# Residual updates of a decoder step: work moved from GpSimd to VectorE and handed out behind the critical tiles

## The chip, the cores and the metric

One Trainium2 chip, one core. The engines that the text names are PE (TensorE: matrix products; PEld is its loading of weights), VectorE (DVE in the rows), ScalarE (ACT), GpSimd (POOL) and SyncE (SP, which only issues DMAs here). Each runs its own instructions strictly in its order; they meet through semaphores. The metric is the device time of one execution in microseconds. Before the change it is 1234.71 us, the median of three runs (1232.79 to 1235.05).

## The reference

One step of a two-layer decoder over 320 tokens (256 of a prompt, 8 times 8 of samples), width 1024. Layer 0 mixes with an S5 state space and a GLU, layer 1 with latent attention (MLA); each layer then attends to 256 memory tokens and applies an MLP. Every sublayer is normalised before and after, and this is what the change touches:

```python
def rms_norm(x, g):
    y = x * lax.rsqrt(jnp.mean(x * x, axis=-1, keepdims=True) + EPS)
    return y * g
...
hp = hp + rms_norm(yp, norm_mix_post[i])
hp = hp + rms_norm(mem_attend(rms_norm(hp, norm_mem_pre[i]), mk, mv, w_mem_q[i], w_mem_o[i]), norm_mem_post[i])
hp = hp + rms_norm(sq_relu_mlp(rms_norm(hp, norm_mlp_pre[i]), w_mlp_up[i], w_mlp_down[i]), norm_mlp_post[i])
```

So between two dense stages stands: a norm of the output y, an addition to the residual h, and the norm of the new h, whose result the next stage multiplies by its weights.

## The kernel before

**Layout.** Activations lie transposed, channels on 128 partitions and the 320 tokens along the row, in KD = 8 tiles j of 128 x 320. Products keep nearly full float32 precision by three matmuls: weights and activations are each split into a rounded high part and a remainder, and `mm3` (L202) adds high x high, high x low and low x high. The activations of a stage are thus `xh` and `xl`, the weights `whi` and `wlo`. `load_chunk` (L178) brings a chunk of 128 x 1024 weights by SyncE's queue into `wraw`, makes `whi` on ScalarE (L190) and `wlo` on VectorE (L191), or on GpSimd for the chunks numbered 3 and 5 after an update (`POOL_LO`, L85). `dense` (L208) goes over groups of up to four output blocks, for each over the chunks of the contraction, and then has a function `evac` take the sums out of PSUM.

**Update.** After the last matmul of a stage, the sum of the squares of its output gives, through a matmul with ones (`ss`) and a square root on ScalarE, the tile `rt` (root of the mean square, one value per token). Four of the five updates are `update_scaled` (L263). It doesn't divide by rt, but works with the residual times rt: for each j it makes the product t_up = h x rt (L272; VectorE for j = 0 and 1, GpSimd for the other six), the sum s = y x gain + t_up (L274, VectorE, written over y), xh = s x gain (L278, ScalarE; L276, VectorE, for j = 0) and xl (L279, VectorE). PE can start on tile j of the next stage when xh and xl of that tile are there. The scale rt goes out again in the next norm. For that, the squares of s (`stat_add`, L111: squares on ScalarE, additions on GpSimd, L118) are summed, `ex` (L284) is the epsilon times rt squared, and `next_root` (L294) makes the root. Where h is needed later (`restore`), it is made as s divided by rt: a reciprocal on VectorE (L160) and eight products on GpSimd (L289). The fifth is `update` (L249), in front of the latent stage of MLA: it divides by rt at once, and the root of the new h (L261) follows in it.

**The five stretches.** They are called A to E here. A is the update after the GLU, in front of the memory query of layer 0 (from 228 us on in the trace). B follows the memory attention, in front of the MLP of layer 0 (361 us). C is `update` after that MLP, in front of MLA (614 us). D follows MLA, in front of the memory query of layer 1 (855 us), and E is in front of the last MLP (979 us); E restores nothing and instead turns h into rows by token as filler work for PE. PE has other filler work too: transposes of cached keys (`kt`, copied to `ktb` by VectorE, L1107, and ScalarE) in A and D, the keys and values of the memory of layer 1 in B.

**What sets the order.** The program is written as a sequence of operations, and a scheduler puts each engine's instructions into an order by the times that it reckons for them. `tc.issue_after(x)` holds back the operations inside it until x has been issued in that reckoning. `self.hold` uses it for weight chunks: chunk n waits in the order for the instruction that is put down for it. In the memory query (`mem_attention`, L1112) the root of h is wanted only for the softmax scale `rsc` (L1165), and stands in before behind the first of two groups, four blocks wide (L1154). In the MLP (`mlp`, L1280) it is wanted after the first half (L1304); there `evac` squares the relu (L1297) and makes `hl` (L1298).

Of the kernel before, what the change touches and what calls it, by code (L numbers as in the profile page):

```python
# [84 lines left out]
POOL_LO = (3, 5)  # L85
# [3 lines left out]
class Trunk:  # L89
# [88 lines left out]
    def load_chunk(self, srcs, cols):  # L178
# [12 lines left out]
        (nc.gpsimd if self.chunk in POOL_LO else nc.vector).tensor_sub(lo[:, :cols], raw[:, :cols], hi[:, :cols].bitcast(F32))  # L191
        return hi, lo

# [55 lines left out]
    def update(self, y, rt, gpost, stat=True):  # L249
# [3 lines left out]
        st = self.stat_new()  # L253
        for j in range(KD):
            t = self.small("t_up", bufs=2)
            (nc.vector if j < 2 else nc.gpsimd).tensor_mul(t, y[:, j, :], r)  # L256
            nc.vector.scalar_tensor_tensor(h[:, j, :], t, gpost(j), h[:, j, :], op0=ALU.mult, op1=ALU.add)  # L257
            if stat:
                self.stat_add(st, h[:, j, :], nc.gpsimd)
        if stat:  # L260
            self.r_next, self.rt_next = self.rsqrt(self.stat_sum(st), D)  # L261

    def update_scaled(self, y, rt, gpost, gpre, restore=True):  # L263
# [4 lines left out]
        self.chunk, self.hold, self.first_sum = 0, {3: self.gate}, self.summed  # L268
        st = self.stat_new()
        for j in range(KD):  # L270
            t = self.small("t_up", bufs=2)
            scaled = (nc.vector if j < 2 else nc.gpsimd).tensor_mul(t, h[:, j, :], rt)  # L272
            s = y[:, j, :]
            nc.vector.scalar_tensor_tensor(s, s, gpost(j), t, op0=ALU.mult, op1=ALU.add)  # L274
            if j == 0:
                nc.vector.tensor_scalar(xh[:, j, :], s, gpre(j), None, op0=ALU.mult)  # L276
            else:
                nc.scalar.activation(xh[:, j, :], s, AF.Copy, scale=gpre(j))  # L278
            lo = nc.vector.scalar_tensor_tensor(xl[:, j, :], s, gpre(j), xh[:, j, :].bitcast(F32),  # L279
                                                op0=ALU.mult, op1=ALU.subtract)  # L280
            self.stat_add(st, s, nc.gpsimd)
        with self.tc.issue_after(lo.ins):
            ex = self.small("w_r", bufs=1)
            nc.vector.scalar_tensor_tensor(ex, rt, EPS, rt, op0=ALU.mult, op1=ALU.mult)  # L284
            r = self.inverse(rt) if restore else None
        if restore:
            with self.tc.issue_after(scaled.ins):
                for j in range(KD):
                    nc.gpsimd.tensor_mul(h[:, j, :], y[:, j, :], r)  # L289
        self.pending = st, ex  # L290
        if not restore:
            self.fillers = self.h_to_tokens(y, rt)

    def next_root(self):  # L294

        st, ex = self.pending
# [19 lines left out]
    def build(self):  # L316
        tc, nc, I, O = self.tc, self.nc, self.I, self.O
        with ExitStack() as ctx:
# [11 lines left out]
            self.fillers = []  # L330
            cp = self.cp
# [1471 lines left out]
```

## Time and profile before

| | |
|---|---|
| median of the runs | 1234.71 us (1232.79 to 1235.05) |
| the profiled execution | 1235.15 us, of which the span of the profile is 1233.5 us |
| PE busy | 1139.3 us, 92% of the span |
| PE weight load busy | 1026.6 us, 83% |
| VectorE busy | 726.7 us, 59% |
| ScalarE busy | 546.7 us, 44% |
| GpSimd busy | 182.3 us, 15%, 190 instructions |
| mean granted clock of PE | 0.966 of full speed |

The shares are means over the whole span, and the stages differ. GpSimd is idle for most of it and dense in the five stretches. PE waits little elsewhere, so its idle time there and the few stretches in which its granted clock was half of the full one are what an update can cost. In the rows further below, a square bracket behind an instruction gives the idle time of its engine just before it and, behind the arrow, the instruction that ended that idle time.

### The profile page before, as it was taken

How to read it: one execution, taken by the hardware profiler on the slowest of the kernel's cores; microseconds unless marked ns; L12 is line 12 of the kernel's file. 1: busy time of each engine (PE TensorE's matmuls, PEld its weight loads, DVE VectorE, ACT ScalarE, POOL GpSimd, SP SyncE). 2: the span in 40 equal slices, each digit the busy share in tenths (PEclk: the TensorE clock that was granted, in tenths of full speed). 3: DMA queues.
4: the chain of work that ended last, by engine and by line, in shares of the span. 5: the costliest groups of instructions: out<-in, count | busy, mean ns of one | idle time of the engine just before them, and what ended most of it. 6: DMA issues, size and time to landing. Idle time of an engine off the chain costs nothing.

```text
span 1233.5 us, 21037 instructions
## 1 busy us (share of the span) xinstructions
PE 1139.3 (92%) x8105; PEld 1026.6 (83%) x8105; DVE 726.7 (59%) x1266; ACT 546.7 (44%) x992; POOL 182.3 (15%) x190
## 2 busy tenths in 40 slices
PE   4997699889988999999989999998999899999996
PEld 3886599776787999999979984578967899999996
DVE  5998944664468553564587674416843685435543
ACT  6344454534444543453366353224443365335541
POOL 2000000350027000000050054202700140000011
PEclk8999799999998999999999999989999999999998
DMA  8535358637334445454443565437272434454441
GB/s 165 180 100 116 72 118 289 245 120 269 124 103 126 137 154 153 143 151 152 154 143 104 170 185 153 140 137 268 84 272 94 137 99 144 151 153 139 155 149 49
DMA packets 151233, 184.84 MB, mean 150 GB/s; under 512 B 16719, under 2 KB 119388, under 8 KB 151068
## 3 DMA queue, kind: packets, MB, share of 16 engines
q1 hardware_dynamic: 141660, 174.84, 46.3%
q10 hardware_dynamic: 6976, 5.46, 1.4%
q0 software_dynamic: 2496, 3.20, 0.9%
q8 instruction: 64, 1.05, 0.3%
q14 instruction: 37, 0.30, 0.1%
HBM read 174.89 MB, written 6.21 MB: 147 GB/s over the span
## 4 chain that ended last, share of the span: by engine, by line
PE 75%; DVE 10%; DMA 5%; SPq 3%; issue 2%; ACT 2%; POOL 2%; POOLq 0%; DVEq 0%; ACTq 0%
PE mm L205 17%; PE mm L204 17%; PE mm L206 17%; PE kt L102 2%; PE sps L1182 2%; PE mm L567 2%; DVE xl L279 2%; PE s L1662 2%; SPq L944 2%; DVE wlo L191 1%; DMA natc<-in_ssm_c_im 1%; PE pov L1239 1%; PE s L1703 1%; PE pps L1217 1%; PE mm L569 1%
## 5 line engine op out<-in xcount | busy, mean ns | idle before, releaser
L191 DVE TENSOR_TENSOR wlo<-wraw,whi 128x1024 fp32r<-128x1024 f32 (+1 forms) x206 | 252.9, 1232 | 279.3 <-ACT whi L190 269.1
L190 ACT ACTIVATE whi<-wraw 128x1024 fp32r<-128x1024 f32 (+1 forms) x216 | 224.5, 1044 | 302.8 <-PE mm L205 246.6
L205 PE MATMUL mm<-xl,whi 128*128 128x320 f32 x944 | 296.8, 317 | 9.1 <-DVE xl L279 7.0
L204 PE MATMUL mm<-xh,whi 128*128 128x320 f32 x944 | 280.6, 318 | 12.7 <-ACT t_up L1295 3.6
L206 PE MATMUL mm<-xh,wlo 128*128 128x320 f32 x944 | 287.3, 314 | 0.0
L205 PEld LDWEIGHTS mm<-xl,whi 128*128 128x128 f32 x944 | 181.8, 193 | 13.7 <-DVE xl L279 9.6
L204 PEld LDWEIGHTS mm<-xh,whi 128*128 128x128 f32 x944 | 175.9, 192 | 16.8 <-ACT t_up L1295 3.9
L206 PEld LDWEIGHTS mm<-xh,wlo 128*128 128x128 f32 x944 | 179.7, 192 | 0.1
L204 PE MATMUL mm<-hh,whi 128*128 128x320 f32 x512 | 158.2, 309 | 0.0
L205 PE MATMUL mm<-hl,whi 128*128 128x320 f32 x512 | 158.0, 309 | 0.0
L206 PE MATMUL mm<-hh,wlo 128*128 128x320 f32 x512 | 157.1, 308 | 0.0
L205 PEld LDWEIGHTS mm<-hl,whi 128*128 128x128 f32 x512 | 96.1, 188 | 0.0
L204 PEld LDWEIGHTS mm<-hh,whi 128*128 128x128 f32 x512 | 96.1, 188 | 0.0
L206 PEld LDWEIGHTS mm<-hh,wlo 128*128 128x128 f32 x512 | 95.9, 188 | 0.0
L118 POOL TENSOR_TENSOR sq<-sq 128x320 f32<-128x320 f32 x34 | 41.4, 1219 | 204.1 <-ACT sq L120 203.4
L191 POOL TENSOR_TENSOR wlo<-wraw,whi 128x1024 fp32r<-128x1024 f32 x10 | 25.4, 2538 | 286.4 <-ACT whi L190 198.1
L102 PEld LDWEIGHTS kt<-ident,kn 128*128 128x128 f32 x256 | 28.9, 143 | 22.2 <-issue 5.8
L102 PE MATMUL kt<-ident,kn 128*128 128x128 f32 x256 | 38.1, 283 | 8.6 <-ACT ktb L1109 3.2
L1591 POOL DMA_DIRECT2D rop<-in_cache_k_rope x64 | 34.5, 540 | 37.4 <-issue 20.4
L256 POOL TENSOR_TENSOR t_up<-y,rr 128x320 f32<-128x320 f32 x6 | 7.5, 1258 | 219.2 <-DVE h L257 219.2
L1107 DVE COPY ktb<-kt 128x512 f32<-128x512 f32 x32 | 22.0, 687 | 21.0 <-PE kt L102 20.9
L1109 ACT ACTIVATE ktb<-kt 128x512 f32<-128x512 f32 x32 | 19.1, 596 | 31.4 <-PE kt L102 26.0
(495 smaller groups left out, 1958.6 us busy)
## 6 DMA issues: line engine op xcount, KB each, us to landing
wraw<-in_w_mlp_up SPq DMA_DIRECT2D x64, 512.0 KB, 4.2
wraw<-in_w_mlp_down SPq DMA_DIRECT2D x64, 512.0 KB, 3.5
kn<-in_cache_mem_k SPq DMA_DIRECT2D x16, 1024.0 KB, 7.3
vn<-in_cache_mem_v SPq DMA_DIRECT2D x16, 1024.0 KB, 9.1
wraw<-in_w_glu SPq DMA_DIRECT2D x32, 256.0 KB, 4.1
wraw<-in_w_mem_q SPq DMA_DIRECT2D x16, 512.0 KB, 5.3
wraw<-in_w_mem_o SPq DMA_DIRECT2D x16, 512.0 KB, 5.0
lat<-in_cache_kv_latent SPq DMA_DIRECT2D x64, 128.0 KB, 2.5
```

The costliest lines, as they stand in the source:

```text
L102: self.nc.tensor.transpose(out, in_, self.ident[b:b + k, b:b + k])
L118: eng.tensor_add(st['acc'], st['acc'], st['last'])
L190: nc.scalar.activation(hi[:, :cols], raw[:, :cols], AF.Copy)
L191: (nc.gpsimd if self.chunk in POOL_LO else nc.vector).tensor_sub(lo[:, :cols], raw[:, :cols], hi[:, :cols].bitcast(F32))
L204: nc.tensor.matmul(ps, wh, xh, start=start, stop=False)
L205: nc.tensor.matmul(ps, wh, xl, start=False, stop=False)
L206: nc.tensor.matmul(ps, wl, xh, start=False, stop=stop)
L279: lo = nc.vector.scalar_tensor_tensor(xl[:, j, :], s, gpre(j), xh[:, j, :].bitcast(F32), op0=ALU.mult, op1=ALU.subtract)
L567: nc.tensor.matmul(ps[b][:, :MT], w[:, bs], xh[:, k, :], start=k == 0, stop=k == KD - 1)
L944: nc.sync.dma_start(tt[s * K:(s + 1) * K, s:], kk[:, 0:L - s])
L1182: nc.tensor.matmul(sps[h * 32:(h + 1) * 32, :MT], qm[:, h * 2 + db, j * 128 + i * 32:j * 128 + (i + 1) * 32], ktb[:, h * 2 + db, :], start ...
L1591: last[eng] = eng.dma_start(dst, src[bass.ds(v, 1)].rearrange("o p d -> (o p) d"))
```

## The change

Nothing of the five updates stays on GpSimd: the products t_up, the additions of squares, the restoring products and the remainders wlo of chunks 3 and 5 all go to VectorE; so do six additions in `finish` (L460) at the end. In `update_scaled` the scaled residual s is written over h instead of over y, and h is restored in place; y is therefore free earlier. `ex`, the additions of squares, the reciprocal and the restoring products are no longer issued on the spot. They go into a list `later`, in the form of functions, and `put_off` issues them, always behind the last xl of the update (`urgent`): four with each weight chunk from number 5 on (7 in the first MLP), the rest in `next_root`. The gate on chunk 3 (the root rt) goes, except in stretch B; instead chunks 3 and 4 (5 and 6 in B) wait in the order for the xl of tiles 2 and 4. In stretch C the sum of squares and the root of h come after the products with `w_kr` in MLA. The diff, cut to what moves work:

```diff
-POOL_LO = (3, 5)
+AFTER = {2: 3, 4: 4}
 TOKENS = (0, 128, SEQ + NS - 128)
...
             nc.scalar.activation(hi[:, :cols], raw[:, :cols], AF.Copy)
-        (nc.gpsimd if self.chunk in POOL_LO else nc.vector).tensor_sub(lo[:, :cols], raw[:, :cols], hi[:, :cols].bitcast(F32))
+        nc.vector.tensor_sub(lo[:, :cols], raw[:, :cols], hi[:, :cols].bitcast(F32))
+        self.put_off(self.rate.get(self.chunk, 0))
         return hi, lo
+    def put_off(self, n=None):
+        while self.later and n != 0:
+            with self.tc.issue_after(self.urgent.ins):
+                self.later.pop(0)()
+            n = n - 1 if n else n
...
-    def update(self, y, rt, gpost, stat=True):
+    def update(self, y, rt, gpost):
...
         r = self.inverse(rt)
+        for j in range(KD):
+            t = self.small("t_up", bufs=2)
+            nc.vector.tensor_mul(t, y[:, j, :], r)
+            nc.vector.scalar_tensor_tensor(h[:, j, :], t, gpost(j), h[:, j, :], op0=ALU.mult, op1=ALU.add)
+    def update_stat(self, last):
+        st = self.stat_new()
+        self.urgent, self.chunk, self.hold, self.rate = last, 0, {}, {1: 3, 2: 3, 3: 2}
+        self.later = [lambda j=j: self.stat_add(st, self.h[:, j, :]) for j in range(KD)]
+        return st
+    def update_scaled(self, y, rt, gpost, gpre, restore=True, skip=0):
+        nc, h = self.nc, self.h
+        xh, xl = self.x = self.xbuf()
+        self.chunk, self.hold, self.first_sum = 0, {3: self.gate} if skip else {}, self.summed
         st = self.stat_new()
...
             t = self.small("t_up", bufs=2)
-            (nc.vector if j < 2 else nc.gpsimd).tensor_mul(t, y[:, j, :], r)
-            nc.vector.scalar_tensor_tensor(h[:, j, :], t, gpost(j), h[:, j, :], op0=ALU.mult, op1=ALU.add)
-            if stat:
-                self.stat_add(st, h[:, j, :], nc.gpsimd)
-        if stat:
-            self.r_next, self.rt_next = self.rsqrt(self.stat_sum(st), D)
-    def update_scaled(self, y, rt, gpost, gpre, restore=True):
-        nc, h = self.nc, self.h
-        xh, xl = self.x = self.xbuf()
-        self.chunk, self.hold, self.first_sum = 0, {3: self.gate}, self.summed
-        st = self.stat_new()
-        for j in range(KD):
-            t = self.small("t_up", bufs=2)
-            scaled = (nc.vector if j < 2 else nc.gpsimd).tensor_mul(t, h[:, j, :], rt)
-            s = y[:, j, :]
-            nc.vector.scalar_tensor_tensor(s, s, gpost(j), t, op0=ALU.mult, op1=ALU.add)
+            nc.vector.tensor_mul(t, h[:, j, :], rt)
+            s = h[:, j, :]
+            nc.vector.scalar_tensor_tensor(s, y[:, j, :], gpost(j), t, op0=ALU.mult, op1=ALU.add)
             if j == 0:
...
                 nc.scalar.activation(xh[:, j, :], s, AF.Copy, scale=gpre(j))
-            lo = nc.vector.scalar_tensor_tensor(xl[:, j, :], s, gpre(j), xh[:, j, :].bitcast(F32),
-                                                op0=ALU.mult, op1=ALU.subtract)
-            self.stat_add(st, s, nc.gpsimd)
-        with self.tc.issue_after(lo.ins):
-            ex = self.small("w_r", bufs=1)
-            nc.vector.scalar_tensor_tensor(ex, rt, EPS, rt, op0=ALU.mult, op1=ALU.mult)
-            r = self.inverse(rt) if restore else None
+            self.urgent = nc.vector.scalar_tensor_tensor(xl[:, j, :], s, gpre(j), xh[:, j, :].bitcast(F32),
+                                                         op0=ALU.mult, op1=ALU.subtract)
+            if j in AFTER:
+                self.hold[AFTER[j] + skip] = self.urgent
+        ex = self.small("w_r", bufs=1)
+        r = self.sm.tile([128, NT], F32, name="rr", tag="rrr", bufs=1)
+        self.later = [lambda: nc.vector.scalar_tensor_tensor(ex, rt, EPS, rt, op0=ALU.mult, op1=ALU.mult)]
+        for j in range(KD):
+            self.later.append(lambda j=j: self.stat_add(st, h[:, j, :]))
         if restore:
-            with self.tc.issue_after(scaled.ins):
-                for j in range(KD):
-                    nc.gpsimd.tensor_mul(h[:, j, :], y[:, j, :], r)
+            self.later.append(lambda: nc.vector.reciprocal(r, rt))
+            for j in range(KD):
+                self.later.append(lambda j=j: nc.vector.tensor_mul(h[:, j, :], h[:, j, :], r))
+        self.rate = {c + skip: 4 for c in range(5, 12)}
         self.pending = st, ex
         if not restore:
-            self.fillers = self.h_to_tokens(y, rt)
+            self.fillers = self.h_to_tokens(h, rt)
...
+        self.put_off()
         st, ex = self.pending
...
             self.fillers = []
+            self.later, self.rate = [], {}
             cp = self.cp
...
             V.tensor_add(y[:, b, :], y[:, b, :], ps)
-            self.stat_add(st, y[:, b, :], nc.gpsimd if b < 6 else None)
+            self.stat_add(st, y[:, b, :])
             yg = self.small("t_up", bufs=2)
...
         else:
-            self.update_scaled(y, rt, self.gain(post, l), self.gain(pre, l), pre != 'norm_mlp_pre' or l == 0)
+            self.update_scaled(y, rt, self.gain(post, l), self.gain(pre, l), pre != 'norm_mlp_pre' or l == 0,
+                               skip=2 * (pre == 'norm_mlp_pre' and l == 0))
         if l == 0 or pre != 'norm_mlp_pre':
...
         h = self.h
-        r, rt = self.r_next, self.rt_next
         mm = lambda name: self.ps_mm.tile([128, 512], F32, name=name, tag="mm")
...
                     A.activation(xh[:, j, :], h[:, j, :], AF.Copy, scale=g(j))
-                    V.scalar_tensor_tensor(xl[:, j, :], h[:, j, :], g(j), xh[:, j, :].bitcast(F32),
-                                           op0=ALU.mult, op1=ALU.subtract)
-                w = self.small("w_r", bufs=1)
-                ex = self.small("ex", bufs=1)
-                V.tensor_mul(w, rt, rt)
-                V.tensor_scalar(ex, w, EPS, None, op0=ALU.mult)
+                    last = V.scalar_tensor_tensor(xl[:, j, :], h[:, j, :], g(j), xh[:, j, :].bitcast(F32),
+                                                  op0=ALU.mult, op1=ALU.subtract)
+                hst = self.update_stat(last)
                 st = self.stat_new()
...
                     self.mm3(ps[:, :NT], hi[:, s], lo[:, s], xh[:, k, :], xl[:, k, :], k == 0, k == KD - 1)
+                self.put_off()
+                r, rt = self.rsqrt(self.stat_sum(hst), D)
+                w = self.small("w_r", bufs=1)
+                ex = self.small("ex", bufs=1)
+                V.tensor_mul(w, rt, rt)
+                V.tensor_scalar(ex, w, EPS, None, op0=ALU.mult)
                 kraw = m1.tile([128, NT], F32, name="kraw", tag="qnh", bufs=1)
```

The line numbers of the order rows below are those of each kernel's own file (L284 of the kernel after is L274 of before, L289 is L279, L282 is L272, L302 is the restoring product). VectorE in stretch A, before: from the first sum y to the fifth pair of remainders; the products t_up of tiles 2 to 7 are on GpSimd.

```order
L1107 COPY ktb<-kt 128x512
L274 SCALAR_TENSOR_TENSOR y<-y,gT,t_up 128x320 x2
L276 TENSOR_SCALAR xh<-y,gT 128x320
L1107 COPY ktb<-kt 128x512
L279 SCALAR_TENSOR_TENSOR xl<-y,gT,xh 128x320 x2
L274 SCALAR_TENSOR_TENSOR y<-y,gT,t_up 128x320 x2
L279 SCALAR_TENSOR_TENSOR xl<-y,gT,xh 128x320 x2
L274 SCALAR_TENSOR_TENSOR y<-y,gT,t_up 128x320 x2
L191 TENSOR_TENSOR wlo<-wraw,whi 128x1024
L279 SCALAR_TENSOR_TENSOR xl<-y,gT,xh 128x320 x2
L274 SCALAR_TENSOR_TENSOR y<-y,gT,t_up 128x320 x2
L279 SCALAR_TENSOR_TENSOR xl<-y,gT,xh 128x320 x2
```

The same place after, where the sum is written to h:

```order
L282 TENSOR_TENSOR t_up<-h,rt 128x320 x2
L289 SCALAR_TENSOR_TENSOR xl<-h,gT,xh 128x320 x2
L284 SCALAR_TENSOR_TENSOR h<-y,gT,t_up 128x320 x2
L282 TENSOR_TENSOR t_up<-h,rt 128x320 x2
L289 SCALAR_TENSOR_TENSOR xl<-h,gT,xh 128x320
L284 SCALAR_TENSOR_TENSOR h<-y,gT,t_up 128x320 x2
L289 SCALAR_TENSOR_TENSOR xl<-h,gT,xh 128x320
L282 TENSOR_TENSOR t_up<-h,rt 128x320 x2
L289 SCALAR_TENSOR_TENSOR xl<-h,gT,xh 128x320
L284 SCALAR_TENSOR_TENSOR h<-y,gT,t_up 128x320
L191 TENSOR_TENSOR wlo<-wraw,whi 128x1024
L284 SCALAR_TENSOR_TENSOR h<-y,gT,t_up 128x320
```

The products now stand in VectorE's row in pairs, each ahead of the sums that use it, and one more wlo (formerly GpSimd's) stands between the sums. VectorE in stretch B, before, from the last remainders xl to the first evacuations of the MLP (t_up and hl):

```order
L279 SCALAR_TENSOR_TENSOR xl<-ymem,gT,xh 128x320 x2
L284 SCALAR_TENSOR_TENSOR w_r<-rt 128x320
L160 RECIPROCAL rr<-rt 128x320
L191 TENSOR_TENSOR wlo<-wraw,whi 128x1024 x2
L154 SCALAR_TENSOR_TENSOR rv<-ss,w_r 128x320
L1307 TENSOR_TENSOR w_r<-rt 128x320
L1308 SCALAR_TENSOR_TENSOR ex<-w_r 128x320
L1297 TENSOR_TENSOR t_up<-t_up 128x320 x2
L1298 TENSOR_TENSOR hl<-t_up,hh 128x320 x2
L1297 TENSOR_TENSOR t_up<-t_up 128x320 x2
L1298 TENSOR_TENSOR hl<-t_up,hh 128x320 x2
```

And after, from `ex` on:

```order
L296 SCALAR_TENSOR_TENSOR w_r<-rt 128x320
L118 TENSOR_TENSOR sq<-sq 128x320
L300 RECIPROCAL rr<-rt 128x320
L118 TENSOR_TENSOR sq<-sq 128x320
L191 TENSOR_TENSOR wlo<-wraw,whi 128x1024
L302 TENSOR_TENSOR h<-h,rr 128x320 x4
L118 TENSOR_TENSOR sq<-sq 128x320
L1314 TENSOR_TENSOR t_up<-t_up 128x320
L302 TENSOR_TENSOR h<-h,rr 128x320
L191 TENSOR_TENSOR wlo<-wraw,whi 128x1024
L1314 TENSOR_TENSOR t_up<-t_up 128x320
L118 TENSOR_TENSOR sq<-sq 128x320
```

The reciprocal moved behind `ex` and one addition, restoring products (h) and additions (sq) stand between the remainders wlo and among the evacuations, and rv, for which the sum of squares has to be complete, is no longer among these rows. ScalarE in stretch A, before, from the last squares of the update to the preparation of the weights for the output projection:

```order
L120 ACTIVATE sq<-y 128x320 x2
L190 ACTIVATE whi<-wraw 128x1024
L1142 ACTIVATE q<-mm 128x256 x2
L190 ACTIVATE whi<-wraw 128x1024
L155 ACTIVATE rt<-rv 128x320
L143 ACT_TABLE_LOAD
L143 ACTIVATE rb<-eps 128x1
L190 ACTIVATE whi<-wraw 128x1024
L1142 ACTIVATE q<-mm 128x256 x2
L190 ACTIVATE whi<-wraw 128x1024 x3
```

And after:

```order
L190 ACTIVATE whi<-wraw 128x1024
L120 ACTIVATE sq<-h 128x320
L190 ACTIVATE whi<-wraw 128x1024
L120 ACTIVATE sq<-h 128x320 x2
L1158 ACTIVATE q<-mm 128x256 x2
L190 ACTIVATE whi<-wraw 128x1024 x3
L155 ACTIVATE rt<-rv 128x320
L143 ACT_TABLE_LOAD
L143 ACTIVATE rb<-eps 128x1
```

The root rt and the table load behind it moved from a place ahead of the last four whi to one behind them, and the last squares went in between the whi.

## Rows read from the trace of the kernel before

**Rows 1.** Busy us (count) of PE, PEld, DVE, ACT, POOL, then PEclk, by chain

```profile
233.10:253.90 20.80, 14.45 (x94) 13.26 (x95) 20.63 (x24) 10.28 (x20) 18.05 (x14) 1.00 0.49 159
361.80:387.10 25.30, 19.80 (x109) 18.22 (x108) 21.79 (x23) 13.41 (x24) 19.17 (x14) 0.80 0.39 115
616.80:636.10 19.30, 17.35 (x123) 15.46 (x122) 18.88 (x22) 12.71 (x24) 16.77 (x16) 1.00 0.44 126
856.80:879.30 22.50, 17.17 (x108) 16.35 (x109) 21.70 (x25) 10.72 (x21) 18.18 (x14) 0.92 0.49 167
980.00:1001.00 21.00, 16.88 (x98) 15.24 (x98) 20.58 (x22) 11.55 (x21) 18.22 (x14) 0.84 0.17 51
```

**Rows 2.** The same columns where the granted clock was half

```profile
254.42:257.83 3.41, 3.41 (x15) 3.41 (x14) 2.65 (x2) 0.00 (x0) 0.92 (x2) 0.50 0.16 55
367.10:377.30 10.20, 8.27 (x30) 7.43 (x31) 9.45 (x9) 3.43 (x7) 8.88 (x7) 0.50 0.60 182
397.80:404.60 6.80, 5.40 (x20) 5.40 (x21) 3.64 (x6) 1.59 (x4) 1.59 (x2) 0.50 0.00 0
```

**Rows 3.** Timeline of VectorE in stretch A: start, us, instruction

```profile
234.50 2.50 DVE L274 SCALAR_TENSOR_TENSOR y<-y,gT,t_up 128x320 f32<-128x320 f32 x2
```

**Rows 4.** Timeline of GpSimd in stretch A

```profile
233.65 2.54 POOL L191 TENSOR_TENSOR wlo<-wraw,whi 128x1024 fp32r<-128x1024 f32 x1 [64.36 <-ACT whi L190]
```

**Rows 5.** Timeline of VectorE after stretch C, GpSimd idle

```profile
641.08 2.15 DVE L160 RECIPROCAL rr<-rt 128x320 f32<-128x320 f32 x1
...
645.26 1.21 DVE L191 TENSOR_TENSOR wlo<-wraw,whi 128x1024 fp32r<-128x1024 f32 x1
646.39 0.54 DVE L1425 SCALAR_TENSOR_TENSOR xl<-h,gT,xh 128x320 fp32r<-128x320 f32 x1
646.85 0.48 DVE L1365 TENSOR_TENSOR kfull<-kraw,cos 128x320 f32<-128x320 f32 x1
647.25 1.01 DVE L1425 SCALAR_TENSOR_TENSOR xl<-h,gT,xh 128x320 fp32r<-128x320 f32 x2
```

**Rows 6.** VectorE's groups in stretch A's chain, GpSimd working: busy, mean ns

```profile
L274 DVE SCALAR_TENSOR_TENSOR y<-y,gT,t_up 128x320 f32<-128x320 f32 x8 | 8.9, 1152 | 0.0
L276 DVE TENSOR_SCALAR xh<-y,gT 128x320 fp32r<-128x320 f32 x1 | 1.0, 977 | 0.0
```

**Rows 7.** Groups over the whole span: busy, mean ns

```profile
L272 POOL TENSOR_TENSOR t_up<-h,rt 128x320 f32<-128x320 f32 x24 | 26.0, 1102 | 7.6 <-DVE y L274 5.0 <-DVE ymem L274 2.6
L1107 DVE COPY ktb<-kt 128x512 f32<-128x512 f32 x32 | 22.0, 687 | 21.0 <-PE kt L102 20.9
```

**Rows 8.** Timeline of PE, pieces after its waits in stretches A, B, E

```profile
253.51 0.41 PE L205 MATMUL mm<-xl,whi 128*128 128x320 f32 x1 [2.05 <-DVE xl L279]
261.38 0.38 PE L204 MATMUL mm<-xh,whi 128*128 128x320 f32 x1 [2.07 <-DVE qm L1145]
367.03 0.69 PE L102 MATMUL kps<-ident,kt 128*128 128x128 f32 x2 [2.74 <-ACT kt L586]
399.20 0.64 PE L204 MATMUL mm<-xh,whi 128*128 128x320 f32 x1 [3.62 <-ACT t_up L1295]
984.06 0.69 PE L102 MATMUL hps<-ident,ymem 128*128 128x128 f32 x2 [1.86 <-DVE ymem L274]
```

**Rows 9.** PE without a wait: 96 matmuls of the memory query

```profile
261.40:275.60 14.20, 14.20 (x96) 14.03 (x96) 5.46 (x13) 3.40 (x5) 5.55 (x6) 1.00 0.54 186
```

**Rows 10.** Timeline of ScalarE after the memory queries of both layers

```profile
276.01 2.94 ACT L190 ACTIVATE whi<-wraw 128x1024 fp32r<-128x1024 f32 x3
...
898.34 1.06 ACT L190 ACTIVATE whi<-wraw 128x1024 fp32r<-128x1024 f32 x1 [1.29 <-DMA wraw<-in_w_mem_o]
```

**Rows 11.** SyncE's queue, then GpSimd, in stretch D: start, us, instruction

```profile
891.85 0.37 SPq L1132 DMA_DIRECT2D v<-out  x1
...
881.83 9.99 POOL L289 TENSOR_TENSOR h<-y,rr 128x320 f32<-128x320 f32 x8 [3.01 <-DVE rr L160]
```

**Rows 12.** Timeline of VectorE at the end of stretch B

```profile
397.53 2.21 DVE L1298 TENSOR_TENSOR hl<-t_up,hh 128x320 fp32r<-128x320 f32 x2
```

## The prediction, made before the change was run

> **What bounds the kernel now.** I read the page's shares first: PE is busy for 92% of the span, so a change beside it gains only where PE stands idle or runs at half clock. Next came windows over the five chains (from the first product t_up to the last xl). In them VectorE is busy for 103.6 of 108.9 us, GpSimd for 90.4, and PE idles 20.80 − 14.45 = 6.35 us in A, 5.50 in B, 1.95 in C, 5.33 in D and 4.12 in E, 23.25 in all [rows 1]. So VectorE's chain of products, sums and remainders ends last there, and PE takes each tile as it comes: the wait of 2.05 us on an xl in A and that of 1.86 on a sum in E are such [rows 8]. The granted clock is the second loss. In B it was half for 10.20 us inside the chain, after PE had waited 2.74 us at 367.0, and for 6.80 us from 397.8 on, around a wait of 3.62 us; behind A's chain for 3.41 us [rows 2, 8]. At 0.5 a stretch loses half its length (5.1, 3.4 and 1.7 us). By the mean clocks of rows 1, D loses 22.5 × 0.08 = 1.8 us and E 21 × 0.16 = 3.4.
>
> Third, why VectorE is slow there. A sum took 1152 ns in the mean in A's chain, the same form 0.54 us after stretch C with GpSimd idle [rows 5, 6]. A pair of sums took 2.50 us from 234.50 on while a wlo of GpSimd ran from 233.65 to 236.19 [rows 3, 4]; GpSimd's products took 1102 ns [rows 7]. So operations with two inputs of the two engines seem to exclude one another, and the time of one is added to the other's.
>
> **Part by part.** Prices on VectorE alone are read from start to start [rows 5]: a remainder or sum 0.46 us (646.39 to 646.85), a product 0.40 (to 647.25), a wlo 1.13 (645.26 to 646.39), a reciprocal 2.15. A ktb copy stays at 0.69 [rows 7]. The xh of tile 0 took 977 ns [rows 6]; its price without GpSimd isn't shown. It lies between the 0.40 of the cheapest row and 0.98; I take 0.4, the nearest form, and the four of them can cost 2.3 us more. By the diff VectorE takes over 30 products, 34 additions and 24 restoring products (88 × 0.40 = 35.2 us) and ten wlo (11.3). These 46.5 us of GpSimd work are not all on the path: only what stands ahead of the last xl is.
>
> The Trainium skill has a page "SBUF — State Buffer", whose section "Who interferes with whom" says that GpSimd has no port of its own but VectorE's second pair, which is taken as an exclusive lock. By that rule the pair of 2.50 us is the lock, which goes with GpSimd's work. If 1.15 us were VectorE's own price of a sum or remainder, the five chains would each hold 18.4 us of these instead of 7.36 and grow by 21.6 us in all, 1257. Rows 5 speak for the lock.
>
> *A.* Eight products 3.20, sixteen sums and remainders 7.36, xh 0.4, two copies 1.38, three wlo 3.39: 15.7 instead of 20.8, 5.1 sooner, within PE's 6.35 idle. Of the half clock behind it I let 0.7 of 1.7 go, since PE comes to it with shorter waits: −5.8. The wait of 2.07 on PSUM at 261.4 [rows 8] had a slow wlo on VectorE ahead of it, −0.7. Given back: the root is now behind the three whi of 2.94 us [rows 10] on ScalarE and behind wlo's on VectorE; `rsc` and the row of roots are wanted by the softmax, and everything of it is queued behind. Nothing of this is in the trace of before. The wait costs between 0 (transposes of keys fill it) and 2.94 + three wlo 3.39 = 6.3 us. I take 1.5 and 0.9, nearer to nothing since filler work stands by, as rows 9 show PE going 14.2 us without a wait in the group ahead. Sum −4.1.
>
> *B.* 3.20 + 7.36 + 0.4 + five wlo 5.65 = 16.6 instead of 25.3, 8.6 sooner, within 5.50 idle + 5.1 clock. The evacuation stall of 3.62 us comes from squares and remainders at 2.21 us a pair, beside restoring products [rows 8, 12]; on VectorE alone a pair takes about 0.9, and 1.1 of the stall goes, because restoring products stand among them now. PE resumes 9.7 sooner, but the square sum has moved behind that point: two products of 320 columns, between 0.69 us (two of 128 columns [rows 8]) and 2.5 times that; I take 1.24, midway. Of the half clock after it 2.7 of 3.4 goes; of the one inside the chain I keep 2.6 of 5.1, because PE's wait for the first tile (2.74 us) stays. −9.7 + 1.24 − 2.7 + 2.6 = −8.6.
>
> *C.* 3.20 + 7.36 + three wlo 3.39 = 14.0 instead of 19.3, but PE idles only 1.95 there. The root of h now comes behind the products with w_kr, whose kraw waits for it; PE has the next stage's tiles in hand. Between 0 and 7.5 us (seven additions 2.8, reciprocal 2.15, sums, root and scale 2.5, the last an estimate by the same forms), I take 1.0: −1.0.
>
> *D.* 3.20 + 7.36 + 0.4 + 1.38 + four wlo 4.52 = 16.9 instead of 22.5, 5.6 sooner. Of PE's 5.33 idle I count 3.6, because C shows that a chain's length isn't all inherited. Here `v` was loaded at 891.85 only when GpSimd's last restoring product (881.83 + 9.99) had let go of the place of y; SyncE's queue stood, the weights of the output projection came late, and ScalarE waited 1.29 us for them [rows 10, 11]. With s in h, y is free earlier: −1.1. The same given back as in A (1.5 and 0.9), and 0.4 for squares that now stand between whi: −1.9.
>
> *E.* 3.20 + 7.36 + 0.4 + 1.13 = 12.1 instead of 21, but four of PE's idle microseconds are short waits for first tiles. The 1.86 goes, and 0.6 of the others; the clock I leave: −2.5.
>
> Sum: 4.1 + 8.6 + 1.0 + 1.9 + 2.5 = 18.1. The profiled execution took 1235.15 us (span 1233.5), 0.4 over the median of the runs, so I forecast 1217.
>
> Hidden: the deferred work of A and D (`ex` 0.4, seven additions 2.8, reciprocal 2.15, eight products 3.2: 8.6 us) lies beside the query's second group, 14.2 us of PE [rows 9]; the six additions in `finish` cost VectorE 2.4 us under PE's last projections. Price without that cover: the slower rival.
>
> **Rivals.** *The clock stays* (lower gain). The half-clock stretches come again wherever PE waits for a first tile, and a chain in front of it doesn't change that. Then A's 0.7, B's 2.7 and 2.5 and D's 1.8 aren't earned: 7.7 less, 1225. For: in E two waits with half clock may well remain; against: B's second stretch hangs on a wait that the lock made.
>
> *All idle time goes* (higher gain). 23.25 of idle time, B's 5.1 and A's 1.7 of clock: 30, 1205. For: E's chain shortens by 8.9 us, over twice PE's idle time there; against: the given-back waits, and C, where 1.95 is all there is.
>
> *Nothing comes of it.* The change may shift PE's waits onto transfers and evacuations of the same length; the wait on DMA in D is one [rows 10]. 1233 to 1237.
>
> *Slower: VectorE becomes the bound behind the chains.* The deferred 8.6 us plus four wlo (4.5) and the copies out of PSUM (some 3.3, estimated from rows 7) make 16.4 us against the 14.2 of PE's work in a group [rows 9]. What is handed out then sits in VectorE's row ahead of a wlo or an evacuation that PE wants, and the sum of squares, later than before, ends last at the softmax: 2.7 each in A and D, 6 in B (8.6 of deferred work ahead of the evacuations, less 2.5 that PE waits there anyway), 7.5 in C (its upper end), and 6.8 for two more half-clock stretches as in rows 2. 25.7 − 18.1 gives 1243. It decides once the waits behind the chains exceed 18.1 us, 3.6 a stretch. For: VectorE was busy for 95% of the chains; against: 46.5 us replace at least as much time that the lock had cost it.
>
> The Trainium skill's page "Perfetto Trace Analysis", section "Optimizing Scalar/DVE Operations", says that when VectorE is saturated, offloading even to GpSimd may make sense, though a shared port may spoil it. Read the first way it speaks against this change and for the slower rival; rows 3 and 4 are the second half of it.
>
> **How the numbers follow.** Forecast 0.52 (1210 to 1223), clock stays 0.20, all idle time goes 0.13, nothing 0.05, slower 0.10. The range that leaves 2 in 10 out would be 1205 to 1228; I open it to 1203 (chains as short as computed, in E too) and to 1231 (the upper ends of the softmax waits, 6.3 each in A and D instead of 2.4, would bring 1225; C's root at its upper end 6.5 more, 1231). Faster by over 0.2% (2.5 us, about what a measurement can tell from no change) holds for the first three and for 0.01 of the slower case, where its waits stop short: 0.86; within it 0.05; slower 0.09.
>
> **What would show it.** In the profile after: GpSimd near idle in the five stretches; sums at about 0.54 us, chains of 14 to 17 us (E 12); the wait of 3.62 in B near 2.5, no half clock behind it; `v` loaded before the restoring products; new waits of PE on `rsc` or ScalarE at the softmax, up to 2.4 each. The forecast is wrong if sums stay near 1 us without GpSimd; if PE's waits at softmaxes, at kraw and at B's evacuations together pass 18 us; or if the half-clock stretches in B stand where they were.

## The result, and the profile after

The changed kernel takes 1216.68 us, the median of four runs (1214.72 to 1220.20), against 1233.75 us for four of before: a ratio of 0.9868, 95% interval 0.9838 to 0.9897. 1217 had been forecast. The time is right; the terms of its sum are not, and most of what follows is about that. First the page of the profile after (busy time, share, instructions); this execution took 1220.2 us:

```profile
span 1218.6 us, 21008 instructions
...
PE 1132.0 (93%) x8105; PEld 1021.1 (84%) x8105; DVE 717.3 (59%) x1364; ACT 546.6 (45%) x992; POOL 54.7 (4%) x92
```

VectorE has taken over 98 operations and is busy for 717.3 us instead of 726.7: what it no longer loses beside GpSimd outweighs the added work. The five chains, as windows with the columns of [rows 1]:

```profile
231.10:245.60 14.50, 12.24 (x84) 11.51 (x84) 14.50 (x31) 7.41 (x13) 0.95 (x1) 1.00 0.58 204
358.20:374.90 16.70, 15.43 (x94) 14.31 (x94) 16.70 (x31) 10.59 (x18) 0.00 (x0) 0.90 0.48 141
601.10:615.40 14.30, 13.91 (x110) 13.70 (x109) 14.29 (x29) 10.71 (x19) 1.76 (x4) 1.00 0.57 162
846.00:860.60 14.60, 13.17 (x92) 12.64 (x93) 14.60 (x31) 7.48 (x14) 0.96 (x1) 1.00 0.70 254
969.00:981.20 12.20, 11.06 (x65) 10.39 (x66) 12.20 (x28) 7.60 (x14) 0.00 (x0) 0.86 0.15 44
```

They last 14.5, 16.7, 14.3, 14.6 and 12.2 us; 15.7, 16.6, 14.0, 16.9 and 12.1 were worked out. VectorE has no gap in them, and PE idles 6.5 us in all instead of 23.25. Its groups in A's chain (busy, mean ns) are at the prices of VectorE alone, where a sum had taken 1152 ns [rows 6]:

```profile
L284 DVE SCALAR_TENSOR_TENSOR h<-y,gT,t_up 128x320 f32<-128x320 f32 x8 | 4.1, 545 | 0.0
L286 DVE TENSOR_SCALAR xh<-h,gT 128x320 fp32r<-128x320 f32 x1 | 0.4, 379 | 0.0
```

**A ledger by stretches.** Both kernels run 8105 matmuls on PE. I took the time at which PE starts its n-th one, in each profile minus that in the first profile of before. The stretches end at n = 1500, 2400, 2900, 4700, 5400, 5600, 6460 and 6700 (221, 354, 443, 705, 815, 850, 973 and 1017 us in before), where PE runs without a wait and the difference stands still; between them and after them it moves by 0.3 us at most, in one experiment (handing out alone) by 0.6. Each column but the first is one profiled execution; "again" is a second one of the same kernel (both in the experiments).

| us | forecast | before again | after | after again |
|---|---|---|---|---|
| ahead of A | 0 | −0.5 | −3.1 | −4.6 |
| A and its attention | −4.1 | 0.0 | −0.5 | −0.6 |
| B | −8.6 | 0.0 | −12.0 | −12.0 |
| C | −1.0 | 0.0 | +7.3 | +4.8 |
| 815 to 850 us | 0 | 0.0 | −4.2 | −4.2 |
| D and its attention | −1.9 | −0.1 | +0.7 | +0.7 |
| E | −2.5 | 0.0 | −3.5 | −3.7 |
| to the end | −18.1 | −0.6 | −15.2 | −19.5 |

A and D gain 8.3 and 5.9 us up to the middle of their attentions (n = 2100 and 6150) and give back 7.8 and 6.6 at the end of them. These are pieces of PE, with its waits; the last, in B, answers to the 3.62 us of [rows 8]:

```profile
303.94 1.99 PE L1255 MATMUL pov<-ptp,v 128*128 128x256 f32 x8
305.77 1.89 PE L1233 MATMUL pps<-kt,q 128*128 128x256 f32 x8
307.59 1.06 PE L1198 MATMUL sps<-ktb,qm 128*32 128x256 f32 x12
311.09 0.44 PE L102 MATMUL ptp<-ident,e 128*128 128x128 f32 x2 [2.44 <-ACT e L1090]
...
322.62 0.58 PE L212 MATMUL mm<-xh,whi 128*128 128x320 f32 x1 [2.13 <-ACT xh L1225]
...
384.92 0.42 PE L212 MATMUL mm<-xh,whi 128*128 128x320 f32 x1 [0.26 <-ACT t_up L1312]
```

The first wait is for the softmax of the second block of samples (`ptp` turns its result), the second for its output, with which the projection begins. D has the same two, 2.44 and 2.35 us. Before, the products for the heads of the prompt (`pov`, `pps`) stood behind the last scores of the samples (`sps`) and covered that softmax; after, they stand ahead of them:

```profile
315.13 1.05 PE L1182 MATMUL sps<-ktb,qm 128*32 128x256 f32 x10
316.11 1.99 PE L1239 MATMUL pov<-ptp,v 128*128 128x256 f32 x8
317.94 1.89 PE L1217 MATMUL pps<-kt,q 128*128 128x256 f32 x8
319.67 0.38 PE L102 MATMUL ptp<-ident,e 128*128 128x128 f32 x2
```

Behind each of A's two waits PE ran for 3.4 us at half the clock (windows as above; the third is of stretch C. The second and third begin 0.1 and 0.8 us ahead of the half clock, so their means are 0.52 and 0.61):

```profile
312.50:315.90 3.40, 3.40 (x24) 1.29 (x26) 0.83 (x2) 0.10 (x1) 0.00 (x0) 0.50 0.00 0
322.60:326.00 3.40, 3.38 (x13) 3.38 (x14) 1.30 (x3) 0.70 (x2) 0.00 (x0) 0.52 0.43 123
622.30:625.70 3.40, 3.38 (x15) 3.39 (x16) 1.50 (x2) 0.77 (x2) 0.00 (x0) 0.61 0.99 293
```

ScalarE's timeline shows why the second wait is long: between the last prompt head's output and that of the samples stands a table load.

```profile
320.09 0.60 ACT L1258 ACTIVATE xh<-pov 128x512 fp32r<-128x512 f32 x1 [0.97 <-PE pov L1255]
320.71 1.28 ACT L136 ACT_TABLE_LOAD   x1
...
322.20 0.36 ACT L1225 ACTIVATE xh<-otp 128x256 fp32r<-128x256 f32 x1
```

In C (third window above) PE waits for the weights of w_kr, 1.49 us on whi and 0.70 on wlo, behind squares and evacuations on ScalarE, and later for two weights of its filler products, 1.05 and 0.76 us; and the reciprocal of the root stands 18 us behind the last xl (which ended at 615.4):

```profile
621.06 0.41 PE L212 MATMUL mm<-xh,whi 128*128 128x320 f32 x1 [1.49 <-ACT whi L190]
622.32 0.41 PE L214 MATMUL mm<-xh,wlo 128*128 128x320 f32 x1 [0.70 <-DVE wlo L191]
...
643.11 0.50 PE L212 MATMUL mm<-whi,mnh 128*128 128x256 f32 x2 [1.05 <-ACT whi L190]
644.37 0.38 PE L213 MATMUL mm<-wlo,mnh 128*128 128x256 f32 x1 [0.76 <-DVE wlo L191]
```

```profile
633.17 2.14 DVE L160 RECIPROCAL rr<-rt 128x320 f32<-128x320 f32 x1
...
635.58 0.48 DVE L1415 TENSOR_TENSOR kraw<-mm,rr 128x320 f32<-128x320 f32 x1
```

Before, it came 5 us behind the last xl, at 641.08 [rows 5]. D's transfer of `v` is no longer held, as SyncE's queue shows; it was issued 34 us earlier than in [rows 11], of which 11 are D's own earlier start, and now within the chain:

```profile
858.01 0.37 SPq L1148 DMA_DIRECT2D v<-out  x1
```

### The profile page after: what moved, and what is told of

It reads as the page before. It is cut to its first block, busy times and chain, and to the rows that moved or that the text cites. A ratio compares the mean times of both kernels' runs of the same rounds, so it can differ in the third digit from the quotient of the medians.

```text
span 1218.6 us, 21008 instructions
## 1 busy us (share of the span) xinstructions
PE 1132.0 (93%) x8105; PEld 1021.1 (84%) x8105; DVE 717.3 (59%) x1364; ACT 546.6 (45%) x992; POOL 54.7 (4%) x92
## 3 DMA queue, kind: packets, MB, share of 16 engines
q8 instruction: 64, 1.05, 0.4%
## 4 chain that ended last, share of the span: by engine, by line
PE 81%; DVE 6%; ACT 4%; DMA 4%; SPq 2%; issue 2%; POOLq 0%; POOL 0%; ACTq 0%; DVEq 0%
PE mm L213 19%; PE mm L212 19%; PE mm L214 19%; PE mm L583 2%; PE kt L102 2%; PE sps L1198 2%; PE s L1681 2%; SPq L960 2%; DVE wlo L191 1%; PE ops L1213 1%; ACT whi L190 1%; DMA wraw<-in_w_mem_k 1%; PE pov L1255 1%; PE s L1722 1%; PE mm L585 1%
## 5 line engine op out<-in xcount | busy, mean ns | idle before, releaser
L191 DVE TENSOR_TENSOR wlo<-wraw,whi 128x1024 fp32r<-128x1024 f32 (+1 forms) x216 | 259.4, 1206 | 277.1 <-ACT whi L190 276.6
L118 DVE TENSOR_TENSOR sq<-sq 128x320 f32<-128x320 f32 x67 | 32.3, 482 | 3.9 <-ACT sq L120 3.0
L1314 DVE TENSOR_TENSOR t_up<-t_up 128x320 f32<-128x320 f32 x64 | 29.8, 486 | 2.1 <-ACT hh L1313 1.9
L1315 DVE TENSOR_TENSOR hl<-t_up,hh 128x320 fp32r<-128x320 f32 x64 | 29.8, 487 | 0.9
L1313 ACT ACTIVATE hh<-t_up 128x320 fp32r<-128x320 f32 x64 | 28.4, 471 | 0.9
```

Source lines behind the costliest of these rows:

```text
L118: eng.tensor_add(st['acc'], st['acc'], st['last'])
L191: nc.vector.tensor_sub(lo[:, :cols], raw[:, :cols], hi[:, :cols].bitcast(F32))
L1313: A.activation(hh[b // 4][:, b % 4, :], a, AF.Square)
L1314: V.tensor_mul(a, a, a)
L1315: V.tensor_sub(hl[b // 4][:, b % 4, :], a, hh[b // 4][:, b % 4, :].bitcast(F32))
```

## The experiments

All but the second profile of before were timed against runs of the kernel before on the same chip.

**Which part of the difference is the change's?** No edit; each kernel once more.

> A second profile of the kernel before. Theory 1: what the two profiles (before, after) differ by outside the five stretches is the change's own doing: PE's 2.6 us between 175 and 200 us (half clock at 196) and the 4.2 us between 814 and 842 us (half clock at 817) come again, and every stretch repeats within 0.5 us. Rival: these two are variations from execution to execution; at least one of the two half-clock stretches is missing here or lies elsewhere, and the span differs by 2 to 5 us for that reason alone.

> The changed kernel again, with a second profile. By PE's count of instructions the first pair of profiles says: A nets -0.5 us, B -12.0, C +7.3, D +0.7, E -3.3, and -7.4 outside. Theory 1: A to E repeat within 1.5 us each, time 1214 to 1220. Rival (the stretches are as noisy as the rest): C or D differs by more than 3 us.

Measured 1234.58 us (one run) and 1216.09 us (1214.99 to 1217.76; ratio 0.9873, 0.9838 to 0.9908). In these two pairs of profiles the stretches repeat within 0.2 us, with one exception: C's +7.3 became +4.8. Its idle time was +3.3 and +2.8, and the half clock of 3.4 us at 623 us did not come again, though the waits ahead of it did (1.49 and 0.70 us both times); a second one, at 650 and 643 us, stands in both. So of C's loss some 2 us hang on where the clock fell. Ahead of A both theories are half right: the half clock at 196 us was missing in the second profile of before, whose start was slower, so that only −0.5 came out. No instruction that the change moves is there; PE waits for a load of cached keys at that point in every profile, 0.97 to 3.19 us. I count none of it as the change's; but all ten profiles of changed kernels lie 0.5 to 4.9 us ahead of the first profile of before there, and why is open. The stretch at 817 us repeated.

**The engine or the handing out?** One kernel does the first alone, one the second:

```diff
(before, engine only)
-POOL_LO = (3, 5)
+POOL_LO = ()
-            scaled = (nc.vector if j < 2 else nc.gpsimd).tensor_mul(t, h[:, j, :], rt)
+            scaled = nc.vector.tensor_mul(t, h[:, j, :], rt)
... (so too the products of update, the additions and the restoring products)
(after, handing out only)
-            nc.vector.tensor_mul(t, h[:, j, :], rt)
+            (nc.vector if j < 2 else nc.gpsimd).tensor_mul(t, h[:, j, :], rt)
... (so too the other operations that had been GpSimd's)
```

> The kernel before with all GpSimd work of the updates on VectorE, nothing deferred: squares are added within the chain, the restoring products follow it at once. Theory 1 (the mutual exclusion of the two engines is what made the chains long): sums take 0.54 us instead of 1.15, chain A about 18 us, and the time is 1221 to 1229, the engine move alone bringing half of the gain or more. Rival (the order of handing out brings it, the engine doesn't matter): sums stay above 0.9 us or VectorE's row gets so long that the time is 1234 or more.

> The kernel after with the same 98 operations on GpSimd as before, but still written over h, bound behind the chain and handed out with later weight chunks. Theory 1: sums beside GpSimd's products take 1.0 us or more again, chain A is 19 to 21 us, and the time is 1229 to 1238. Rival (handing out is what brings the gain): 1222 or less. In between (1223 to 1228) both count.

Measured 1222.93 us (ratio 0.9932, 0.9904 to 0.9960) and 1231.58 us (0.9983, 0.9963 to 1.0003). VectorE's groups in A's chain, engine only:

```profile
L274 DVE SCALAR_TENSOR_TENSOR y<-y,gT,t_up 128x320 f32<-128x320 f32 x8 | 4.3, 538 | 0.0
...
L118 DVE TENSOR_TENSOR sq<-sq 128x320 f32<-128x320 f32 x6 | 2.9, 475 | 0.0
```

And handing out only, VectorE first and GpSimd's second:

```profile
L284 DVE SCALAR_TENSOR_TENSOR h<-y,gT,t_up 128x320 f32<-128x320 f32 x8 | 7.3, 926 | 0.0
```

```profile
L282 POOL TENSOR_TENSOR t_up<-h,rt 128x320 f32<-128x320 f32 x6 | 6.5, 1082 | 2.8 <-DVE h L284 2.8
```

The form that takes 538 ns without GpSimd takes 926 beside it: the price is the engine's, as forecast. The length of the chains takes both halves. The five of them last 18.0, 20.2, 16.9, 18.2 and 16.9 us with the engine only, 19.1, 25.3, 19.7, 18.9 and 17.1 with the handing out only; of the 36.7 us that both together take off, the first alone takes 18.6 and the second 8.8. By the ledger, engine only: A +0.2, B −9.9, C +2.3, D −0.3, E −2.3. Handing out only: A −3.2, B −5.1, C +16.0, D −4.2, E −1.2. So B is mostly the engine's. In A and D the engine alone brings nothing, since `ex`, the reciprocal, the eight restoring products and a wlo now stand in VectorE's row between the last xl and the copies that free PSUM, and PE waits for these (A; 2.42 us in D):

```profile
249.51 2.13 DVE L160 RECIPROCAL rr<-rt 128x320 f32<-128x320 f32 x1
251.68 3.30 DVE L289 TENSOR_TENSOR h<-y,rr 128x320 f32<-128x320 f32 x8
254.90 1.22 DVE L191 TENSOR_TENSOR wlo<-wraw,whi 128x1024 fp32r<-128x1024 f32 x1
...
256.37 0.21 DVE L1145 COPY qm<-mm 128x64 f32<-128x64 f32 x1
```

```profile
256.73 0.60 PE L204 MATMUL mm<-xh,whi 128*128 128x320 f32 x1 [4.08 <-DVE qm L1145]
```

The handing out alone gains more in A and D than both together, because the give-back at the end of the attention is missing there (0.76 us of waiting, as before). What C loses in that kernel is more than in any other, and it eats what the other stretches gain: PE's idle time in C grew by 7.8 us, with waits of up to 2.08 us on a wlo of GpSimd, and 17.1 us of it ran at half clock. Why those waits come was not followed further.

**What gives back A and D?** The first kernel binds the three whi that stand ahead of the root on ScalarE behind it. The second binds only the table load behind the last output of the samples; PE's order stays as it is, and on ScalarE only the rows about that place move.

```diff
(root first)
                 rt = self.next_root()
+            self.hold.update({c: self.gate for c in (9, 10, 11)})
(table last)
-        with self.tc.issue_after(self.last_exp.ins):
+        with self.tc.issue_after(self.last_exp.ins), self.tc.issue_after((self.last_otp or self.last_exp).ins):
...
-                A.activation(hi, src, AF.Copy)
+                self.last_otp = A.activation(hi, src, AF.Copy)
```

> The kernel after, with the three whi behind the memory query (chunks 9 to 11) bound in the order behind the root rt, so that rt and the table load come first on ScalarE in A and D. In the schedule this also puts the last sample block's output (otp) ahead of the last prompt head, as in the kernel before. Theory 1 (the late root, by the order that it brings at the attention's end, is what gives back 7.8 us in A and 6.6 in D): A and D keep their 8.3 and 5.8, time 1201 to 1206. Rival (the late root costs no more than its own wait of 0.86 us per layer, and the attention's end is slow for another reason): 1213 to 1216.

> The kernel after, with the table load for the next square root (L136) also bound behind the last xh<-otp of the attention; PE's order is the same, ScalarE's changes in that place alone. Theory 1 (of what A and D give back, the wait of 2.13 and 2.35 us at the output projection is the table load of 1.28 us and two small activations, and the half clock of 3.4 us behind it hangs on it): the waits fall to 0.4 to 0.8 us, time 1209 to 1213.5. Rival (the wait is the softmax's own and only changes its name): 1215 to 1218.

Measured 1205.50 us (1203.75 to 1208.18; ratio 0.9788, 0.9745 to 0.9832) and 1214.90 us (1210.58 to 1218.73; 0.9880, 0.9834 to 0.9926). ScalarE with the root first:

```profile
269.12 0.47 ACT L155 ACTIVATE rt<-rv 128x320 f32<-128x320 f32 x1 [1.22 <-DVE rv L154]
...
271.01 2.93 ACT L190 ACTIVATE whi<-wraw 128x1024 fp32r<-128x1024 f32 x3
...
319.01 0.38 ACT L1226 ACTIVATE xh<-otp 128x256 fp32r<-128x256 f32 x1
321.15 0.60 ACT L1259 ACTIVATE xh<-pov 128x512 fp32r<-128x512 f32 x1 [1.76 <-PE pov L1256]
321.76 1.28 ACT L136 ACT_TABLE_LOAD   x1
```

The samples' output now comes ahead of the last head's, and of the two waits one of 0.76 us is left. On PE the order at the attention's end is that of before again. The ledger has A −6.4 and D −5.3 instead of −0.5 and +0.7, nothing given back. Up to the middle of A it gains 6.4 instead of 8.3; 3.4 us at half clock, at 232 us and so ahead of the edit's place, are in this profile and not in that of after. With the table last the samples' output stays last, and only the second wait is cut, from 2.13 to 0.52 and from 2.35 to 0.74 us:

```profile
320.02 0.42 PE L212 MATMUL mm<-xh,whi 128*128 128x320 f32 x1 [0.52 <-ACT xh L1225]
```

The half clock behind it is gone, in D the one behind the first wait too: A −3.3, D −3.9. In its profile that is 7.4 us of the give-back. The timed runs show little of it: 1214.90 lies between the bound that I had set (1213.5) and the rival's (1215), the profiled run, 1210.58, was its fastest, and the interval, some 1212 to 1224 us, reaches from a loss of 7 us against after to a gain of 4. The waits are settled, their worth in time is not. The root's own wait, for which the forecast had put 1.5 and 0.9 us, is 0.86 us in after (on rsc, in A and in D).

**What loses C?** C undone as a whole, and C on VectorE but on the spot:

```diff
(C as before; the squares and the root are again made in update)
...
+            (nc.vector if j < 2 else nc.gpsimd).tensor_mul(t, y[:, j, :], r)
...
+            self.stat_add(st, h[:, j, :], nc.gpsimd)
+        self.r_next, self.rt_next = self.rsqrt(self.stat_sum(st), D)
...
-                hst = self.update_stat(last)
...
-                self.put_off()
-                r, rt = self.rsqrt(self.stat_sum(hst), D)
(C on VectorE: the same with nc.vector in the first line, and without nc.gpsimd in the second)
```

> The kernel after, with stretch C as in the kernel before: GpSimd makes six products and the additions, the root of h is made within the update. Theory 1 (C's loss of 4.8 to 7.3 us is the late root and the squares handed out among MLA's weights): C comes to within 1 us of before, time 1209 to 1212.5. Rival (C loses because PE comes there earlier and meets its fillers and their weights at another place, whatever C's update does): C stays at +4 or more, 1215 to 1219.

> As the run before, but C's products and additions on VectorE, issued on the spot, with the root in the update: only the handing out is undone in C. Theory 1 (handing out and the late root cost in C, the engine doesn't): C at 0 to +2.5, time 1210 to 1214. Rival (the engine move itself costs in C, since PE idles only 1.95 us there and VectorE's row gets longer): C at +4 or more, 1215 to 1219.

Measured 1213.59 us (1207.91 to 1216.94; ratio 0.9850, 0.9796 to 0.9904) and 1213.80 us (1209.70 to 1219.57; 0.9858, 0.9801 to 0.9916). The ledger has C at +1.0 and +2.3, against +4.8 and +7.3: handing out with the late root is what costs most; the two are undone together here, and which of them costs is not shown. The traces part the waits. Those of 1.05 and 0.76 us on the filler's weights go in both kernels. Those on w_kr go only with GpSimd; with C's work on VectorE they stand, on the spot too, in this kernel, in "engine only" (1.79 and 1.21) and in the last one below (1.79 and 1.14):

```profile
621.90 0.41 PE L212 MATMUL mm<-xh,whi 128*128 128x320 f32 x1 [1.79 <-ACT whi L190]
623.51 0.63 PE L214 MATMUL mm<-xh,wlo 128*128 128x320 f32 x1 [1.06 <-DVE wlo L191]
```

So the engine move by itself costs C something as well. The times lie a little above the first bound and within the second; the intervals alone would not separate them from after. A warning on the ledger comes from here too: in A these two kernels have the order of after on PE, VectorE, ScalarE and GpSimd, and yet −1.4 and −1.7 us instead of −0.5, with the half clock in other places.

**Both together.** The edit of "root first" with C as before, and with C on VectorE:

> The kernel after with both edits: the three whi behind the root in A and D, and stretch C as in the kernel before (GpSimd's products and additions, root in the update). Theory (the two losses are independent, each in its own stretch): A -6.5, B -12.5, C +1, D -5.3, E -3.6 and the half clock at 817 us gone or not (4.2): time 1200 to 1205, below the 1205.5 of the first edit alone. Rival (they aren't additive: an earlier C only meets later waits): 1205 to 1209.

> The same with C's work on VectorE on the spot. Theory (in C the engine hardly matters, the late root does): C at +2, time 1201 to 1206, within 2 us of the run before. Rival (C wants GpSimd): over 1206.

Measured 1204.00 us (1201.16 to 1206.19; ratio 0.9775, 0.9747 to 0.9803) and, for the second, a ratio of 0.9811 (0.9779 to 0.9842); one of its runs stood at 5303.82 us, for which no profile shows a reason, and the five others at 1202.21 to 1212.38, median 1206.98, just above the bound of the theory, where the rival begins. The first is the fastest kernel here. Its ledger: A −6.4, B −12.8, C 0.0, 815 to 850 us −4.2, D −5.2, E −4.0, −34.0 to the end with −1.4 ahead of A; by stretches the two losses are independent. By the median it beats "root first" alone by 1.5 us, less than a comparison can tell. C's engine is not settled by the times, whose intervals overlap; in the profiles VectorE costs 1.2 us more than GpSimd in both pairs (+1.2 and 0.0 here, +2.3 and +1.0 above), with the waits on w_kr.

## Why the prediction came out right, and where it was wrong

**The lock and the chains: right.** Sums at 545 ns, the five chain lengths within 2.3 us, three of them within 0.3; the two halves of the change show that GpSimd's work lengthens VectorE's instructions (926 and 538 ns). xh took 379 ns, so the end of 0.98 us is out. The Trainium skill's rule of the lock ("SBUF — State Buffer", "Who interferes with whom") agrees with 926 against 538 ns of one form; its opposite, 1257 us, did not come.

**B: right in kind, too small.** −12.0 instead of −8.6. The evacuation stall fell from 3.62 to 0.26 us, not to 2.5, and the half clock inside the chain from 10.2 to 3.4 us. I had kept 2.6 us of it because of a wait of 2.74 us that I thought would stay; 0.71 us of it is left.

**A and D: the gain was too small, the give-back was the failed step.** A's 6.5 and D's 4.7 without what they give back measured 8.3 and 5.9. I let A and D give back 2.4 us each for a root that is late at the softmax (and D 0.4 for squares); its own wait was 0.86. But 7.8 and 6.6 went at the other end of the attention. What failed is the step that prices the late root by a wait where the softmax begins, with transposes of keys to fill it. With the root's place the scheduler had changed the orders behind it: on PE the last scores of the samples stood behind the prompt's products instead of ahead of them, which left nothing to cover their softmax (2.44 us), and on ScalarE the samples' output stood behind the last head and behind a table load (2.13 us in A, 2.35 in D). Transposes that ran out don't account for it: by the middle of A PE has done 108 of them in after, 110 before and with the root first, where PE comes to the same place 6.4 us sooner than before and gives nothing back. The order in the rows of ScalarE shows the second wait beforehand; I had compared it at the query only. The slower rival named the softmax as the place, at 2.7 each.

**C: the mis-sized term.** −1.0 was worked out from 1.95 of idle time less 1.0 for a late root, between 0 and 7.5. It was +4.8 and +7.3, near the end that the slower rival took. I had PE with "the next stage's tiles in hand"; behind the last xl it ran filler products and then waited for the weights of w_kr and later for those of the filler, 4.0 us in all. PE's idle time and the half clock make up most of the loss: 3.3 and 3.4 of the +7.3 (two stretches of 3.4 us at half clock, taken as 1.7 each), 2.8 and 1.7 of the +4.8.

**E: right in kind, too small.** −3.5 and −3.7 instead of −2.5. PE's idle time fell by 2.2 us, about what I had counted; the rest is the clock that I had left, with 3.4 us at half clock instead of 6.8. **Outside the steps:** −4.2 at 817 us, where PE's waits didn't change. Before, and the same place after:

```profile
817.60:827.80 10.20, 9.51 (x42) 9.33 (x41) 0.69 (x1) 0.60 (x1) 0.00 (x0) 0.50 0.55 200
```

```profile
809.30:819.50 10.20, 9.51 (x69) 9.24 (x69) 2.38 (x3) 2.10 (x3) 0.00 (x0) 1.00 0.69 254
```

PE is busy for 9.51 of 10.2 us in both, at half clock in the one. It came in both profiles of before and in "engine only", in part in "C on VectorE", and in none of the other eight profiles. "C on VectorE" has the order of after on PE, VectorE, ScalarE and GpSimd there, so this order alone doesn't decide it. Why is open, and the 4.2 us can't be put down to the change. So 1217 came out by offsets, which is luck: B, E and this stretch gained 8.6 to 8.8 us more than I had counted, A, C and D lost 12 to 14.5 us more, and the rest, 3.1 to 4.6 us, fell ahead of A.

**Slips in the sums.** The rival of the clock takes off 1.8 us in D that D's sum doesn't hold; without them it stands at 1223, not 1225. An update has six additions of squares, not seven, and `finish` gave VectorE four, not six: 34 in all, as counted there. None of this moves the forecast.

## What to carry to other kernels

Moving work off an engine that slows the critical one's instructions pays where the critical chain stands, as long as what is moved doesn't then stand ahead of a copy that the next matmul waits for; so try each half of such a change by itself, stage by stage. When something is handed out later, follow the order of every engine to the stage's end: a root, a table load or a square in another place decides there who comes last, and whether the filler still stands where the wait is. Check a forecast by stretches, against a second profile of both kernels, before taking a right total for a right explanation.

## What the runs showed that I had not expected

The waits of a stretch repeat within some 0.2 us between two profiles of one kernel, C's apart (0.5 us), while the half clock comes and goes at places where no wait differs: at 817 us, worth 4.2 us, and at 623 us in one of two profiles of the same kernel, some 2 us. A short table load of 1.28 us in the wrong place cost 1.6 us of waiting in each attention, and in that profile half clock of 3.4 us behind it.
